# A two-layer decoder trunk on one core: layer 0's embedding gate as seven block products instead of eight

## The chip, the cores and the metric

The kernel runs on one core of one Trainium2 chip, in one launch. The metric is the time of a run on the device in microseconds (us); a kernel's time is the median of its runs.

## The reference, cut to what matters

512 tokens of width 1024 pass two layers. Each layer has a mixer (attention with a short convolution in layer 0, gated linear attention in layer 1), a gated MLP with a causal convolution, and a last stage that adds a gated projection of a per-layer input `p[i]` (512 x 256). All is float32.

```python
def _per_layer_embedding(x, p_i, norm, w_gate, w_proj):
    gate = jax.nn.sigmoid(_rms_norm(x, norm) @ w_gate)      # 512x1024 @ 1024x1024
    return gate * (p_i @ w_proj)                            # 512x256 @ 256x1024
...
    x = x + _conv_ffn(_rms_norm(x, ffn_norm[i]), ...)       # up 1024 -> 5632, down 2816 -> 1024
    x = x + _per_layer_embedding(x, p[i], ple_norm[i], ple_w_gate[i], ple_w_proj[i])
```

## The kernel before, in words

**Layout.** The residual `xT` is kept transposed: eight tiles `xT[0..7]` of 128 features by 512 tokens. A product of float32 numbers is made of three TensorE matmuls: every operand is split into a high part (a copy rounded to the matmul's type, on ScalarE) and a low part (the rest, a subtraction on VectorE), and high x high, high x low and low x high are summed in PSUM (`mm3`; `split` and `cut` make the parts). The factor 1/rms of a token is the same for all features, so it is applied after the product (`R`, 1/rms spread over 128 partitions). The sum of squares is gathered in `acc` (a square on ScalarE, an addition on VectorE, by feature tile), then `end_norm` turns it by four PE transposes, reduces it on VectorE and takes the root on GpSimd (`r`), and `spread` turns `r` back by four transposes into `R`.

**Seven products.** The MLPs already use Strassen's scheme in places: with weights cut in 2 x 2 blocks by even and odd feature tile and by column tile, and tokens cut in two halves of 256, the product of a pair of output tiles takes seven block products instead of eight. `seven(...)` is a generator with four steps: step 1 makes the product with `e1` (even features, left tokens) and copies it into both results X and Y; step 2 makes the ones with `s1`, `o1`, `s2`; step 3 the one with `s3`; step 4 those with `s4` and `o2`. Each of the seven is `product`: 4 j x 3 matmuls of 256 columns. `s1` to `s4` are sums of token halves, and on the weight side `seven_forms` makes the sums: it cuts the plain blocks (`plain`), subtracts in place, cuts the result (`t13`), subtracts, cuts a narrow one (`t2`, into two buffers of the tag `sq`, of which there are two), subtracts; step 3 cuts the last one (`last`, from `od`).

**The first MLP** (`ffn`, with its pool `fp`) ends with `down`, the down-projection, in units of two output tiles. On TensorE its order is written out (`manual_schedule`); the other engines' orders are chosen by a scheduler at compile time, which takes the ready instruction that comes first in the program. When the tiles of a unit are final, `finish(m)` is called for them. In layer 0 that was `advance`: split `gain * xT[m]` into `xg[m]`, and add its square to `acc`. In layer 1 it is `blocks`: it scales two tiles, forms `e1`, `o1`, `o2` and `s1` to `s4` of the pair, and splits them. Unit 3 is last; after the units 0 to 2 are final, 84 matmuls of 512 columns of it are left.

**The last stage of layer 0** (`ple0`) had a pool of its own. For each of four pairs of output tiles it cut a panel of `ple_w_gate` and one of `ple_w_proj`, made 2 x 8 x 3 matmuls of 512 columns for the gate and 2 x 2 x 3 for the projection, multiplied by `R`, took the sigmoid, multiplied, added to `xT` and called `advance` with the next layer's gain. Its TensorE order was left to the scheduler. The next mixer begins with products of `xg` with `gla_w_in` (`Values`), and these too are left to the scheduler.

Of the kernel before, what the change touches and what calls it, by code (L numbers as in the profile page):

```python
# [63 lines left out]
class Kernel:  # L64
# [228 lines left out]
    def blocks(self, m, gain, scratch, tags):  # L293


        nc = self.nc
        H = S // 2
        gx = scratch()
        nc.scalar.activation(gx, self.xT[m], AF.Copy, scale=gain[:, m : m + 1])

        def parts(x):
            w = x.shape[1]
            h, l = self.pair(self.fp, *tags)
            self.split((h[:, :w], l[:, :w]), x)
            return lambda b, c: (h[:, b * H + c * P : b * H + (c + 1) * P], l[:, b * H + c * P : b * H + (c + 1) * P])

        if m % 2 == 0:
            self.even = gx
            self.e1 = parts(gx[:, :H])
        else:  # L310
            e, o = self.even, gx
            op = parts(o)
            s12, s34 = scratch(), scratch()
            nc.vector.tensor_tensor(s12[:, :H], e[:, H:], o[:, H:], ALU.add)
            nc.vector.tensor_tensor(s12[:, H:], s12[:, :H], e[:, :H], ALU.subtract)
            s12p = parts(s12)
            nc.vector.tensor_tensor(s34[:, :H], e[:, :H], e[:, H:], ALU.subtract)
            nc.vector.tensor_tensor(s34[:, H:], o[:, :H], s12[:, H:], ALU.subtract)
            s34p = parts(s34)
            e1 = self.e1  # L320
            at = lambda f, b: lambda c: f(b, c)
            self.forms.append(
                dict(e1=at(e1, 0), o1=at(op, 0), o2=at(op, 1), s1=at(s12p, 0), s2=at(s12p, 1), s3=at(s34p, 0),
                     s4=at(s34p, 1))
            )
        self.squares(m)

# [459 lines left out]
    def operand(self, m, gain, tags):  # L787
# [19 lines left out]
            self.forms.append([(out[:, q, c], out[:, q + 1, c]) for q in (0, 2) for c in (slice(0, H), slice(H, S))])  # L807
        self.squares(m)

    def by_parity(self, raw):  # L810

        rv = raw.rearrange("p (j u) n -> p j u n", u=2)
        return rv[:, :, 0], rv[:, :, 1]
# [46 lines left out]
        nc.vector.tensor_tensor(b21, b21, b11, ALU.subtract)  # L860
        return t2

    def seven(self, od, ws, xg, forms, keep=True):

        nc = self.nc
        H = S // 2
        mm = nc.tensor.matmul
        W, V = self.pa(), self.pa()[:, :H]  # L870
        X, Y = self.ps(), self.ps()
        plain, t13, t2 = ws

        def product(out, w, c, x, first=False):
            kw = dict(skip_group_check=True)
            for j in range(ND // 2):
                (wh, wl), (xh, xl) = w(j, c), x(j)
                mm(out, wh, xh, start=first and j == 0, stop=False, **kw)  # L878
                mm(out, wh, xl, start=False, stop=False, **kw)  # L879
                mm(out, wl, xh, start=False, stop=j == ND // 2 - 1, **kw)  # L880

        def tokens(u, half):
            c = slice(half * H, (half + 1) * H)
            return lambda j: (xg[2 * j + u][0][:, c], xg[2 * j + u][1][:, c])

        s1, s2, s3, s4 = (lambda j, q=q: forms[j][q] for q in range(4))
        left, right = slice(0, H), slice(H, S)
# [4 lines left out]
        product(V, t13, 0, s1, True)  # L892
        more = V
        if keep:
            more = self.sp.tile([P, S], F32, tag="acc", name=self.nm("more"), bufs=1)[:, :H]
            nc.scalar.copy(more, V)
        product(X[:, left], plain, 1, tokens(1, 0))
        product(Y[:, left], t2, 0, s2)
        yield nc.scalar.copy(X[:, right], Y[:, left])
        last = self.cut_blocks(od)  # L900
        product(X[:, right], t13, 1, s3)
        yield nc.scalar.copy(Y[:, right], X[:, right])
        product(Y[:, left], last, 1, s4)
        product(X[:, right], last, 0, tokens(1, 1))
        yield X, Y, more

    def ffn(self, i, project, next_gain):
# [8 lines left out]
        with tc.tile_pool(name=f"ffn{i}", bufs=1) as fp:  # L916
# [47 lines left out]
            def prepare(d, behind=None):  # L964
# [11 lines left out]
                return self.seven(od, ws, xg, self.forms), w0, column(values[0], 0)  # L976

            def begin(d, steps, w):

# [64 lines left out]
            self.begin_norm(mine)  # L1044
            self.forms = []
            xg = self.xg
            ready = []

            def done(m, ps):
# [41 lines left out]

                close()
            self.begin_norm(mine)
            finish = lambda m: self.advance(m, next_gain)
            if i == 1:
                self.forms = []
                halves = []

                def half():
                    if not halves:  # L1100
                        x = both()
                        halves.extend([x[:, 0], x[:, 1]])
                    return halves.pop(0)

                self.half = half
                finish = lambda m: self.blocks(m, next_gain, half, mine if m < 4 else other)
            work = [lambda f=f: split_blocks(f) for f in (14, 16, 18, 20)]
            for f in (8, 10, 12):
                split_pair(f)
            self.down(i, acts, down_forms, both, work, finish, copied)  # L1110
            if i == 0:
                self.end_norm()
            else:
                self.ple1(fp)

    def down(self, i, acts, forms, both, work, finish, copied):
# [10 lines left out]
        if i == 0:  # L1127
            plan += [(2, "A", 0, 4, 3), (2, "A", 4, 6), (3, "B", 0, 4), (3, "B", 4, 8), (3, "A", 0, 3), (3, "A", 3, 6)]
            loads = ["B0", "A0", "A1", "B1", "C0", "B2", "C2", "A2", "B3", "A3"]
            inner = ["C1", "C3"]  # L1130
        else:
            plan += [(2, "A", 0, 3), (2, "A", 3, 6), (3, "B", 0, 4), (3, "B", 4, 8)]
            plan += [(3, "C", 0, 4), (3, "C", 4, 8), (3, "A", 0, 3), (3, "A", 3, 6)]
            loads = ["B0", "A0", "A1", "B1", "C0", "B2", "C2", "A2", "B3", "C3", "A3"]
            inner = ["C1"]
        blocked = 4 - i
        plan = [p if len(p) == 5 else p + (None,) for p in plan]
        got, cuts, gens, pending = {}, {}, {}, []
# [36 lines left out]
        def more_forms(u):  # L1175
# [1 line left out]
            t13 = self.cut_blocks(ev)  # L1177

            def rest():
                gens[u] = self.seven(od, (plain, t13, self.more_forms(ev, od)), acts[14:], forms, False)  # L1180

            pending.append(rest)

# [123 lines left out]
            out.append(hl)  # L1307
        return out

    def ple0(self, next_gain):  # L1310
        nc, a = self.nc, self.a
        with self.tc.tile_pool(name="ple0", bufs=1) as pool:
            xg, R, pT = self.xg, None, None
            wg = a["ple_w_gate"][0].rearrange("(k p) n -> p k n", p=P)
            wp = a["ple_w_proj"][0].rearrange("(k p) n -> p k n", p=P)
            self.begin_norm(("b0", "b1"))

            def finish(m2, w, gates):
                for c in range(2):
                    m, s = m2 + c, gates[c]  # L1320
                    pj = self.ps()
                    for k in range(2):
                        self.mm3(pj, w(k, c * P, (c + 1) * P), pT[k], start=k == 0, stop=k == 1)
                    nc.vector.tensor_tensor(s, s, pj, ALU.mult)
                    nc.vector.tensor_tensor(self.xT[m], self.xT[m], s, ALU.add)
                    self.advance(m, next_gain)

            late = None
            for m2 in range(0, ND, 2):
                g = self.weights(wg[:, :, m2 * P : (m2 + 2) * P], ND, 256)  # L1330
                w = self.weights(wp[:, :, m2 * P : (m2 + 2) * P], 2, 256)
                gates = []
                for c in range(2):
                    pg = self.ps()
                    for k in range(ND):
                        self.mm3(pg, g(k, c * P, (c + 1) * P), xg[k], start=k == 0, stop=k == ND - 1)
                    gates.append(pg)
                if R is None:
                    R = self.spread()
                    pT = self.load_p(0, pool)  # L1340
                for c in range(2):
                    s = pool.tile([P, S], F32, tag="pg", name=self.nm("pg"), bufs=4)
                    nc.vector.tensor_tensor(s, gates[c], R, ALU.mult)
                    nc.scalar.activation(s, s, AF.Sigmoid)
                    gates[c] = s
                if late:
                    finish(*late)
                late = (m2, w, gates)
            finish(*late)
            self.end_norm()  # L1350

    def ple1(self, fp):

# [35 lines left out]
        def add(banks, form, ws, first=False, order=None):  # L1389
# [2 lines left out]
            kw = dict(skip_group_check=True)  # L1392
            both = (0, H)
            for j, i, (c0, c1), o in order or [(j, i, both, banks[i]) for j in range(J) for i in range(2)]:
                lh, ll = forms[j][form](i)
# [607 lines left out]
```

## Time and profile before

| | us |
|---|---|
| runs (3) | 1200.00, 1200.26, 1201.72 |
| median | 1200.26 |
| profiled execution, first to last instruction | 1199.4 |
| of it, down-projection's end, units 0 to 2 final to the last matmul | about 501 to 520.5 |
| layer 0's last stage on TensorE | 520.5 to 576.7 |

The page gives the profiled execution by its span; 0.9 us lie between this span and the median of the runs. Times "at" a number below are us from the span's start. PE is the TensorE's matmuls, PEld its weight loads, DVE VectorE, ACT ScalarE, POOL GpSimd, SP the engine that issues most DMAs. A matmul's own time in the trace overlaps the next one's, so PE's pace is read from the distance of starts.

### The profile page before, as it was taken

What the parts mean: (1) busy time and instruction counts of PE and PEld (TensorE: products, weight loads), DVE (VectorE), ACT (ScalarE), POOL (GpSimd) and SP (SyncE); (2) the same over time, 40 slices, a digit from 0 to 9 for tenths busy, and PEclk for the clock granted to TensorE, in tenths of its full rate; (3) what the DMA queues carried; (4) which work ended last, traced back from release to release, by engine and by line L of the source; (5) the groups of instructions that cost most, each with busy time, mean ns of one, the idle gap of its engine ahead of it and who ended that gap; (6) DMA issues with size and microseconds to landing.
All of it is one profiled execution on the core that took longest, in us unless ns stands there. A gap on an engine that the chain in (4) does not pass through costs nothing.

```text
span 1199.4 us, 19840 instructions
## 1 busy us (share of the span) xinstructions
PE 1192.4 (99%) x8074; PEld 1076.9 (90%) x8074; DVE 966.4 (81%) x1543; ACT 671.1 (56%) x1093; POOL 44.8 (4%) x64
## 2 busy tenths in 40 slices
PE   9999999999999999999999999999999999999998
PEld 8877789999999989888988988899999999888887
DVE  6786687898999986746679876687989999988595
ACT  7466565655565753534563655555555656655374
POOL 2610000000000000000100000000000000000000
PEclk9999999999999999999999999999999999999999
DMA  7232222333332342232322222223233333322601
GB/s 223 72 97 80 74 88 71 106 106 106 106 107 89 113 138 84 87 106 86 107 93 70 75 68 70 88 72 115 97 112 100 106 106 114 124 89 98 210 1 71
DMA packets 113216, 117.74 MB, mean 98 GB/s; under 512 B 2873, under 2 KB 108403, under 8 KB 113125
## 3 DMA queue, kind: packets, MB, share of 16 engines
q1 hardware_dynamic: 111760, 115.35, 29.5%
q8 instruction: 63, 1.03, 0.4%
q0 software_dynamic: 560, 0.42, 0.3%
q10 hardware_dynamic: 804, 0.70, 0.2%
q14 instruction: 29, 0.23, 0.1%
HBM read 114.37 MB, written 2.10 MB: 97 GB/s over the span
## 4 chain that ended last, share of the span: by engine, by line
PE 92%; DVE 5%; ACT 1%; DMA 1%; issue 0%; ACTq 0%; DVEq 0%
PE ps L169 14%; PE ps L170 14%; PE ps L171 14%; PE pa L170 7%; PE pa L171 7%; PE pa L169 7%; PE ps L878 5%; PE ps L880 5%; PE ps L879 5%; PE pa L878 2%; PE pa L880 2%; PE pa L879 2%; PE ps L1400 1%; PE ps L1398 1%; PE ps L1399 1%; DVE wl L150 1%
## 5 line engine op out<-in xcount | busy, mean ns | idle before, releaser
L149 ACT ACTIVATE wh<-raw 128x1024 fp32r<-128x1024 f32 (+4 forms) x154 | 152.5, 992 | 128.9 <-PE ps L170 92.8
L150 DVE TENSOR_TENSOR wl<-raw,wh 128x1024 fp32r<-128x1024 f32 (+4 forms) x154 | 175.3, 1140 | 57.9 <-ACT wh L149 57.0
L825 ACT ACTIVATE wh<-raw 128x1024 fp32r<-128x1024 f32 x78 | 83.0, 1064 | 115.8 <-DVE raw L850 75.9
L937 DVE SCALAR_TENSOR_TENSOR zt<-z,vfa,zt 128x510 f32<-128x510 f32 (+1 forms) x176 | 131.0, 745 | 0.3
L826 DVE TENSOR_TENSOR wl<-raw,wh 128x1024 fp32r<-128x1024 f32 x78 | 95.4, 1222 | 12.8 <-ACT wh L825 12.8
L171 PE MATMUL pa<-b,wl 128*128 128x256 f32 x352 | 97.3, 276 | 0.1
L171 PE MATMUL pa<-a,wl 128*128 128x256 f32 x352 | 97.2, 276 | 0.0
L169 PE MATMUL pa<-b,wh 128*128 128x256 f32 x352 | 97.2, 276 | 0.0
L169 PE MATMUL pa<-a,wh 128*128 128x256 f32 x352 | 97.2, 276 | 0.0
L170 PE MATMUL pa<-b,wh 128*128 128x256 f32 x352 | 97.2, 276 | 0.0
L170 PE MATMUL pa<-a,wh 128*128 128x256 f32 x352 | 97.2, 276 | 0.0
L935 ACT ACTIVATE zt<-z,vfb 128x512 f32<-128x512 f32 x88 | 71.5, 813 | 19.6 <-DVE z L927 9.5
L169 PE MATMUL ps<-b,wh 128*128 128x512 f32 x192 | 76.6, 399 | 0.0
L170 PE MATMUL ps<-b,wh 128*128 128x512 f32 x192 | 75.1, 391 | 0.0
L171 PE MATMUL ps<-b,wl 128*128 128x512 f32 x192 | 75.0, 391 | 0.0
L171 PEld LDWEIGHTS pa<-b,wl 128*128 128x128 f32 x352 | 66.1, 188 | 0.3 <-DVE wl L150 0.3
L169 PEld LDWEIGHTS pa<-b,wh 128*128 128x128 f32 x352 | 66.1, 188 | 0.0
L170 PEld LDWEIGHTS pa<-a,wh 128*128 128x128 f32 x352 | 66.1, 188 | 0.0
L169 PEld LDWEIGHTS pa<-a,wh 128*128 128x128 f32 x352 | 66.1, 188 | 0.0
L170 PEld LDWEIGHTS pa<-b,wh 128*128 128x128 f32 x352 | 66.1, 188 | 0.0
L171 PEld LDWEIGHTS pa<-a,wl 128*128 128x128 f32 x352 | 66.1, 188 | 0.0
L878 PE MATMUL ps<-four,wh 128*128 128x256 f32 x232 | 64.7, 279 | 0.0
(472 smaller groups left out, 3667.7 us busy)
## 6 DMA issues: line engine op xcount, KB each, us to landing
raw<-in_ffn_w_up_dram SPq DMA_DIRECT2D x42, 1024.0 KB, 5.1
raw<-in_ffn_w_down_dram SPq DMA_DIRECT2D x13, 1024.0 KB, 4.8
raw<-in_hy_w_in_dram SPq DMA_DIRECT2D x8, 1024.0 KB, 5.0
raw<-in_gla_w_in_dram SPq DMA_DIRECT2D x8, 1024.0 KB, 5.1
raw<-in_ffn_w_down_dram SPq DMA_DIRECT2D x8, 768.0 KB, 4.1
raw<-in_ple_w_gate_dram SPq DMA_DIRECT2D x6, 1024.0 KB, 4.6
raw<-in_hy_w_out_dram SPq DMA_DIRECT2D x16, 256.0 KB, 3.9
raw<-in_gla_w_out_dram SPq DMA_DIRECT2D x4, 1024.0 KB, 4.7
```

Source lines behind the costliest of these rows:

```text
L149: nc.scalar.activation(hv, v, AF.Copy)
L150: self.rest_cut = nc.vector.tensor_tensor(lv, v, hv.bitcast(F32), ALU.subtract)
L169: mm(out, lh, rh, start=start, stop=False, **kw)
L170: mm(out, lh, rl, start=False, stop=False, **kw)
L171: mm(out, ll, rh, start=False, stop=stop, **kw)
L825: nc.scalar.activation(h, src, AF.Copy)
L826: nc.vector.tensor_tensor(l, src, h.bitcast(F32), ALU.subtract)
L878: mm(out, wh, xh, start=first and j == 0, stop=False, **kw)
L879: mm(out, wh, xl, start=False, stop=False, **kw)
L880: mm(out, wl, xh, start=False, stop=j == ND // 2 - 1, **kw)
L935: nc.scalar.activation(y, z, AF.Identity, scale=w2[:, f : f + 1], bias=bb[:, f : f + 1])
L937: nc.vector.scalar_tensor_tensor(out=y[:, tap:], in0=z[:, : S - tap], scalar=w[:, f : f + 1], in1=y[:, tap:], op0=ALU.mult, op1=ALU.add,)
```

## The change: what it does

Layer 0's gate is now computed by `seven`, four groups of two output tiles. `finish` is `blocks` in both layers, so the sums of x are made at the end of the down-projection; `ple0` is called inside `ffn`, uses the pool `fp`, and has its TensorE order written out. `proj` and the turning of `p` (`load_p`) come first, then the groups; `p` is loaded through SP in two halves before the stage (it was one load through ScalarE's queue). All of `ple_w_proj` is loaded and split once. The split of the new `xT` for the next mixer (`enter`) moves from each group to the last one, because its buffers (`b0`, `b1`) hold sums of x until then. `end_norm` stands in group 0 after step 2, `spread` after step 3. `seven` takes its operands by name and a function for the buffer that keeps V; for the MLPs this is only another way of writing.

```diff
@@ blocks @@
-            return lambda b, c: (h[:, b * H + c * P : ...], l[:, b * H + c * P : ...])
+            return [(h[:, c], l[:, c]) for c in HALVES]
...
+                dict(e1=self.e1[0], o1=op[0], o2=op[1], s1=s12p[0], s2=s12p[1], s3=s34p[0], s4=s34p[1])
@@ seven @@
-        product(W[:, left], plain, 0, tokens(0, 0), True)
+        product(W[:, left], plain, 0, x["e1"], True)
...
-        if keep:
-            more = self.sp.tile([P, S], F32, tag="acc", ...)[:, :H]
+        if keep is not None:
+            more = keep()
@@ ffn, behind the up-projection @@
-            finish = lambda m: self.advance(m, next_gain)
-            if i == 1:
-                ...
+            finish = lambda m: self.blocks(m, next_gain, half, mine if m < 4 else other)
...
             if i == 0:
-                self.end_norm()
+                self.ple0(fp, both, self.g_mix[1])
@@ ple0 @@
+        pin = self.p_halves(0)
+        steps = prepare(load(0))          # panel by SP; plain, t13, t2; seven(...)
+        wj_raw = self.raw(2, D)
+        nc.sync.dma_start(wj_raw, a["ple_w_proj"][0].rearrange("(k p) n -> p k n", p=P))
+        wj = [... two tiles of the tag "four" ...]
+        for c in (slice(0, D // 2), slice(D // 2, D)):
+            self.split([w[:, :, c] for w in wj], wj_raw[:, :, c])
...
+        def enter(*ms):
+            for m in ms:
+                hl = self.pair(self.fp, "b0", "b1")
+                self.split(hl, self.xT[m], next_gain[:, m : m + 1])
+                self.xg.append(hl)
+
+        with tc.manual_schedule(engines={ET.PE}):
+            pT = self.load_p(0, fp, pin)
+            pjs = [proj(0), proj(1)]
+            for g in range(groups):
+                ends = g + 1 == groups
+                if not ends:
+                    raw = load(g + 1)
+                next(steps)
+                if ends:
+                    enter(0, 1)
+                next(steps)
+                if ends:
+                    enter(2, 3)
+                if g == 0:
+                    self.end_norm()
+                    self.begin_norm(None)
+                else:
+                    pjs = [proj(2 * g)]
+                next(steps)
+                if g == 0:
+                    R = self.spread()
+                else:
+                    pjs.append(proj(2 * g + 1))
+                last = steps
+                if not ends:
+                    steps = prepare(raw)
+                X, Y, more = next(last)
+                if ends:
+                    enter(4, 5)
+                gates = both()
+                h2 = lambda x: x.rearrange("p (u t) -> p u t", u=2)
+                nc.vector.tensor_tensor(gates[:, 0], X, R, ALU.mult)
+                s = gates[:, 1]
+                nc.vector.tensor_tensor(h2(s), h2(Y), more.unsqueeze(1).to_broadcast([P, 2, H]), ALU.add)
+                nc.vector.tensor_tensor(s, s, R, ALU.mult)
+                for c in range(2):
+                    m, s = 2 * g + c, gates[:, c]
+                    nc.scalar.activation(s, s, AF.Sigmoid)
+                    nc.vector.tensor_tensor(s, s, pjs[c], ALU.mult)
+                    nc.vector.tensor_tensor(self.xT[m], self.xT[m], s, ALU.add)
+                    self.squares(m)
+            enter(6, 7)
+        self.end_norm()
@@ run @@
-        self.ple0(self.g_mix[1])
```

More of the change, by code (lines that the diff above doesn't have):

```diff
@@ L808, in operand, with aside @@
         self.squares(m)
+    def aside(self):
+        return self.sp.tile([P, S], F32, tag="acc", name=self.nm("more"), bufs=1)[:, : S // 2]
     def by_parity(self, raw):
@@ L861, in more_forms, with tokens_and_forms, seven @@
         return t2
-    def seven(self, od, ws, xg, forms, keep=True):
+    def tokens_and_forms(self, xg, forms, first=0):
+        part = lambda u, c: lambda j: tuple(x[:, c] for x in xg[first + 2 * j + u])
+        s1, s2, s3, s4 = (lambda j, q=q: forms[j][q] for q in range(4))
+        left, right = HALVES
+        return dict(e1=part(0, left), o1=part(1, left), o2=part(1, right), s1=s1, s2=s2, s3=s3, s4=s4)
+    def seven(self, od, ws, x, keep=None):
         nc = self.nc
@@ L880, in product @@
                 mm(out, wl, xh, start=False, stop=j == ND // 2 - 1, **kw)
[L882 to L887, printed above, removed]
-        product(W[:, left], plain, 0, tokens(0, 0), True)
+        left, right = HALVES
+        product(W[:, left], plain, 0, x["e1"], True)
         nc.scalar.copy(X[:, left], W[:, left])
@@ L975, in prepare @@
                 values.append(load_values(d))
-                return self.seven(od, ws, xg, self.forms), w0, column(values[0], 0)
+                return self.seven(od, ws, operands, self.aside), w0, column(values[0], 0)
             def begin(d, steps, w):
@@ L1046, in ffn @@
             xg = self.xg
+            operands = self.tokens_and_forms(xg, self.forms)
             ready = []
@@ L1093, in ffn, with half @@
             self.begin_norm(mine)
-            finish = lambda m: self.advance(m, next_gain)
-            if i == 1:
[L1096 to L1106, printed above, removed]
+            self.forms = []
+            halves = []
+            def half():
+                if not halves:
+                    x = both()
+                    halves.extend([x[:, 0], x[:, 1]])
+                return halves.pop(0)
+            self.half = half
+            finish = lambda m: self.blocks(m, next_gain, half, mine if m < 4 else other)
             work = [lambda f=f: split_blocks(f) for f in (14, 16, 18, 20)]
@@ L1308, in load_p @@
         return out
[L1310 to L1318, printed above, removed]
-                for c in range(2):
[L1320 to L1350, printed above, removed]
```

46 lines of the change are left out of this document (32 added, 14 removed).

## The prediction

> **What bounds the kernel now.** I read the page first: the span, each engine's busy share and the chain that ended last.
>
> ```profile
> span 1199.4 us, 19840 instructions
> ...
> PE 1192.4 (99%) x8074; PEld 1076.9 (90%) x8074; DVE 966.4 (81%) x1543; ACT 671.1 (56%) x1093; POOL 44.8 (4%) x64
> ...
> PE 92%; DVE 5%; ACT 1%; DMA 1%; issue 0%; ACTq 0%; DVEq 0%
> ```
>
> The chain is PE's for 92% of the span. So matmul time removed is worth its full price, but only if PE does not wait in exchange. The busy time of stretches shows how things stand around the change: the end of the down-projection, and the old last stage.
>
> ```profile
> 490.00:520.50 30.50, 30.50 (x163) 26.22 (x162) 17.50 (x22) 14.60 (x22) 0.00 (x0) 1.00 0.23 73
> 520.50:576.70 56.20, 56.20 (x257) 46.61 (x256) 34.19 (x50) 26.26 (x38) 1.01 (x1) 1.00 0.32 105
> ```
>
> The columns are the stretch, its length, and busy time of PE, PEld, DVE, ACT and POOL, then the granted clock, which is full. PE is busy throughout both: the old stage has no wait to win back, and every wait of the new one is a loss. DVE has 13 us free in the first stretch and 22 us in the second.
>
> **The change part by part.** First, what PE no longer does. The groups by line, in the window of the old stage, count the gate's matmuls (the same x64 on lines 170 and 171), and the order of time gives the paces.
>
> ```profile
> L169 PE MATMUL ps<-a,wh 128*128 128x512 f32 x64 | 25.1, 392 | 0.0
> ...
> L111 ACT ACTIVATE a<-xT,vec 128x512 fp32r<-128x512 f32 x2 | 1.4, 711 | 0.0
> ```
>
> ```profile
> 520.49 0.39 PE L169 MATMUL ps<-a,wh 128*128 128x512 f32 x1
> ...
> 524.57 0.33 PE L333 MATMUL pa<-cf,acc 128*128 128x128 f32 x1
> ```
>
> ```profile
> 489.09 0.28 PE L878 MATMUL ps<-four,wh 128*128 128x256 f32 x1
> ...
> 490.45 0.28 PE L878 MATMUL ps<-a,t 128*128 128x256 f32 x1
> ```
>
> 18 matmuls of 512 columns lie between the first two starts: 4.08/18 = 0.2267 us each. 12 of 256 columns (one block product of the down-projection) lie between the others: 1.36/12 = 0.1133, half of it. The old gate was 192 x 0.2267 = 43.5 us. The new one is 4 groups x 7 products x 12 x 0.1133 = 38.1. **Saved on PE: 5.4 us.** The projection (48 matmuls) and the sixteen transposes (p, the sums, R) stay.
>
> This half price is the premise. The Trainium skill ("TensorE: Matmul & The Clock Gate", section "Back-to-back issue gap") says otherwise: a stream of load-and-multiply pairs runs at about 131 ns per matmul at 512 columns and 81 at 128, so halving the columns would save far less than half. By its ratio (an estimate: 98 at 256 columns, by interpolation on that page) the new gate would cost 57 us and the change would lose 13. The measured pace contradicts it here, and the sum goes by the pace.
>
> Second, the waits. The new stage's PE order is fixed, so whatever its next instruction waits for holds up all that is queued behind it.
>
> *The head.* The first PE work is now the turning of p, then the projection of tiles 0 and 1, which need p split. The old stage did this in its middle, behind other matmuls. Rows in order of time, of that place and of the down-projection's end:
>
> ```profile
> 520.01 1.37 DVE L1209 TENSOR_TENSOR xT<-xT,ps 128x512 f32<-128x512 f32 x2 [1.31 <-PE ps L171]
> ...
> 520.46 0.63 ACT L149 ACTIVATE wh<-raw 128x512 fp32r<-128x512 f32 x1 [3.02 <-PE ps L170]
> ...
> 532.30 1.04 PE L1304 MATMUL pa<-cf,pin 128*128 128x128 f32 x8
> ...
> 533.33 1.09 ACT L108 ACTIVATE ph<-pa 128x512 fp32r<-128x512 f32 x2
> ...
> 534.13 1.28 DVE L109 TENSOR_TENSOR pl<-pa,ph 128x512 fp32r<-128x512 f32 x2
> ```
>
> With ACT and DVE nearly free, the first low part was done 534.13 + 0.69 - 532.30 = 2.5 us after the transposes began. PE has about 0.8 us of transposes and one matmul on the high part (0.23) in that time, so it waits at least 1.5 us. At the other end, work that comes earlier in the program goes first. Tiles 6 and 7 are final at 521.4 (first row). Their two scaled copies (0.71 each, the L111 row), the splits of `e1` and `o1` (half and full width, about 0.4 and 0.6), and the cut of `last` (about 1.06), whose buffer comes free when the 0.63 us cut of the second row could start, put about 3 us on ACT ahead of p, and `s12`, `s34` and their low parts stand ahead on DVE. Then the low part of p is ready at about 526.4 instead of 523, and PE waits 5.0 us. I take 3.3, the middle: DVE will run late here (below), which delays tiles 6 and 7 themselves and lets p's high parts slip in front. What these waits cover in return is the pair's own sums: they would otherwise hold up the products with `e1` and `s1`. That is free only because of this wait.
>
> *The sums of squares.* `t2` takes both `sq` buffers, and the squares of tiles 6 and 7 come after it, so they wait for step 2's last product. The MLP's start has the same pattern:
>
> ```profile
> 189.81 1.16 ACT L290 ACTIVATE sq<-xT 128x512 f32<-128x512 f32 x2 [0.35 <-PE ps L879]
> ...
> 190.63 1.48 DVE L291 TENSOR_TENSOR acc<-acc,sq 128x512 f32<-128x512 f32 x2
> ...
> 192.39 0.60 PE L333 MATMUL pa<-cf,acc 128*128 128x128 f32 x4
> ...
> 194.01 1.04 POOL L179 TENSOR_TENSOR rtok<-rs,mhalf 128x4 f32<-128x4 f32 x1 [58.48 <-DVE rs L178]
> ```
>
> The squares start when the PE releases them, and `acc` is done at 192.11, 2.3 us later. There 24 matmuls of the value columns filled the time. In the new group 0 the transposes of `acc` follow step 2 directly: PE waits 2.4 us, or nothing if the squares get the buffers before `t2`. I take 2.4, since `t2` can be made before tiles 6 and 7 are final.
>
> *The root.* From the transposes' start to `r` it took 195.05 - 192.39 = 2.7 us. The new order has the transposes (0.36) and step 3 (1.36) in between: PE waits 1.0 us before `spread`.
>
> *DVE.* Rows of one piece each, from the up-projection (groups by line) and a queued pair (order of time):
>
> ```profile
> L826 DVE TENSOR_TENSOR wl<-raw,wh 128x1024 fp32r<-128x1024 f32 x36 | 44.0, 1222 | 4.2 <-ACT wh L825 4.2
> ...
> L800 DVE TENSOR_TENSOR four<-four 128x256 f32<-128x256 f32 x4 | 1.7, 418 | 0.0
> ```
>
> ```profile
> 547.61 1.29 DVE L1325 TENSOR_TENSOR xT<-xT,pg 128x512 f32<-128x512 f32 x2
> ```
>
> Two queued pieces of 512 take 1.29, so one occupies 0.60 in a queue and 0.69 alone; 1024 take 1.13 and 1.22. A group has three wide cuts, and fourteen pieces of 512: four weight differences, one narrow cut, seven in the tail (X and Y to `xT`), two squares. Queued that is 3 x 1.13 + 14 x 0.60 = 11.8 us, beside 84 x 0.1133 + 12 x 0.2267 = 12.2 us on PE. So DVE just fits, with PE waits here and there: 0.2 for groups 1 to 3. The old `advance` is out of groups 0 to 2, and `enter` (8 pieces) falls into the last group and behind it, where `Values` products with tiles 0 to 5 cover it, and the two free banks of X and Y of group 2 let them start: 0.2. Before the stage, sums for tiles 0 to 5 add 3 x (5 x 0.42 + 3 x 0.69 - 2 x 0.69) = 8.3 us (the last two are the old low parts), the first panel 4 x 0.69 more than the old cuts, and the projection's weights 2 x 1.22: 17.5 + 13.5 = 31.0 us in 30.5. No PE work of the down-projection waits for it (its cuts come first in the program), but the head meets a late DVE.
>
> *DMA.* SP issues the two halves of p first; the second waits for the buffer in which activation 7's low part lies. Queued behind it are the first panel and the projection's weights.
>
> ```profile
> raw<-in_ple_w_gate_dram SPq DMA_DIRECT2D x6, 1024.0 KB, 4.6
> ```
>
> After that part is read, 36 matmuls x 0.2267 = 8.2 us remain. If the panel really queues behind, two loads of 4.6 and a cut of 2.3 end 3 us late, inside the long head; if it is asked for when its buffer comes free, they cost nothing. I take nothing.
>
> The sum: -5.4 + 3.3 + 2.4 + 1.0 + 0.4 = **+1.7 us** on the 1199.4 us span, so 1201.1; the median of the runs lies 0.9 above the span: **1202.0**.
>
> **The rivals.**
>
> 1. *Covered.* The squares get `sq` first and the head is at its short end: -5.4 + 1.5 + 1.0 + 0.2 = -2.7, so 1197.6 (1194.9 if PE's work alone counted). For it speaks that DVE is late, which can push `t2` behind the squares; against it the MLP's start, where `t2` was first. Chance 0.22.
> 2. *Long head.* The pair's chain and the cut of `last` go before p: 5.0 instead of 3.3, +3.4, so 1203.7. It is measurably slower than before from a head of 4.0 us on. For it speaks the program order; against it that ACT idled 3.02 us before 520.46. Chance 0.20.
> 3. *DVE becomes the bound.* If pieces come singly, waiting for PE or ACT, a group costs 3 x 1.22 + 14 x 0.69 = 13.3 us, 1.1 over PE's 12.2, in three groups: +3.2 more, 1205.2. Against it: in the old stage's tail the pieces did queue (the pair of 1.29). Chance 0.09.
> 4. *The clock.* At the start of the kernel PE was slow after idling:
>
> ```profile
> 1.31 3.36 PE L204 MATMUL pa<-ones_r 128*128 128x512 f32 x7 [1.31 <-DVE mhalf L193]
> 4.47 1.05 PE L470 MATMUL ps<-cf,xin 128*128 128x128 f32 x4
> ```
>
> Seven matmuls took 3.16, 0.45 each, twice the pace: 1.6 us lost. If the long head sets PE back in this way, 1205.3. The Trainium skill ("TensorE: Matmul & The Clock Gate", Part 1) has a rule for it: an idle window of about 3.4 us halves the clock until PE has been busy as long. No row here shows it in mid-kernel. Chance 0.05.
>
> 5. *Half-width matmuls at the pace of their weight loads.* A load takes 188 ns, 336 of them 63.2 us, 20 more than the old gate: about 1220. The 0.1133 pace speaks against it, and the skill's issue-gap rule above is its only support. Chance 0.02.
>
> **How the numbers follow.** The forecast, 1202.0, has 0.42. For this kernel about 0.2% (2.4 us) is what a measurement tells from no change, so "same" is 1197.9 to 1202.7. Faster: most of rival 1, 0.20. Same: the rest of it, most of the forecast, a little of rival 2: 0.40. Slower: the forecast's upper part and rivals 2 to 5, 0.40. The forecast's own range is 1200.0 to 1203.5. The range to hold 8 in 10 takes in rival 1 nearly to PE's work alone and rivals 2 to 4: 1196.5 to 1206.0.
>
> **What would show it.** Right: gate matmuls 336 at 0.1133; PE idle 2 to 5 us before the first projection matmul, released by the low part of p; 2 to 3 us before the transposes of `acc`, released by DVE; about 1 us before those of `r`, released by POOL; next to nothing in groups 1 to 3. Wrong: squares of tiles 6 and 7 that run before step 2 ends (then 2.4 us less); transposes of p found among the down-projection's matmuls (then the head costs nothing); waits for `wl`, `t` or `raw` in groups 1 to 3 (DVE); `Values` starting late behind the stage.

## The result and the profile after

The changed kernel takes 1211.32 us (median of 4 runs, 1211.22 to 1212.7) against 1200.96 (4 runs, 1200.0 to 1201.72) for the kernel before beside it: ratio 1.0087, 95% interval 1.0073 to 1.0101. The forecast was 1202.0, and the time lies above the top of its range. The profiled execution grew from 1199.4 to 1209.5. Its page, the lines that answer to those shown of before, and the granted clock by slices:

```profile
span 1209.5 us, 20223 instructions
...
PE 1192.0 (99%) x8218; PEld 1081.0 (89%) x8218; DVE 993.3 (82%) x1593; ACT 691.6 (57%) x1135; POOL 45.3 (4%) x64
...
PEclk9999999999999999989999999999999999999999
...
PE 60%; issue 29%; DVE 7%; ACT 2%; DMA 1%; POOL 0%; ACTq 0%; POOLq 0%; DVEq 0%
```

PE's busy time hardly fell, although 5.4 us of gate work are gone: one slice has a lower clock, in which the same matmuls count longer. It is the slice of the changed stage. By stretches (the end of the down-projection, the head of the stage, the rest of it):

```profile
490.00:520.50 30.50, 30.50 (x163) 26.15 (x162) 26.39 (x44) 21.65 (x34) 0.00 (x0) 1.00 0.33 104
...
520.20:534.10 13.90, 6.73 (x22) 4.88 (x21) 10.71 (x19) 6.67 (x12) 0.00 (x0) 0.66 0.36 117
534.10:586.80 52.70, 49.53 (x383) 46.69 (x382) 42.05 (x60) 31.25 (x54) 1.43 (x1) 0.99 0.19 60
```

The down-projection is as long as before, its PE full, though DVE does 26.4 us there in place of 17.5. The stage runs from 520.2 to 586.8: 66.6 us, where the old one took 56.2. These 10.4 us are the whole difference, and most of them are in the first 13.9 us, for which the profile lists only 22 matmuls and transposes.

**The head**, PE in order of time. What is in brackets is idle time and who ended it:

```profile
520.23 1.03 PE L1305 MATMUL pa<-cf,pin 128*128 128x128 f32 x8
525.21 0.79 PE L169 MATMUL pa<-four,four 128*128 128x512 f32 x1 [3.95 <-ACT four L108]
529.23 0.79 PE L170 MATMUL pa<-four,four 128*128 128x512 f32 x1 [3.23 <-DVE four L109]
529.82 0.63 PE L171 MATMUL pa<-four,four 128*128 128x512 f32 x1
...
533.66 0.63 PE L171 MATMUL pa<-four,four 128*128 128x512 f32 x1
534.09 0.41 PE L884 MATMUL pa<-a,wh 128*128 128x256 f32 x1
```

The head's work is 0.8 for the transposes of `p` and 12 x 0.2267 = 2.7 for the projection, 3.5 us. It takes 534.09 - 520.23 = 13.9, so **10.4 us are lost**. By starts, less the work in between: 4.2 before the first projection matmul (for p's high part), 3.8 before the second (for its low part), and the other 2.4 because the matmuls after that follow at (533.66 - 529.82)/9 = 0.427 us, half pace. Who held up `p` stands in VectorE's and ScalarE's rows:

```profile
520.18 1.28 DVE L1210 TENSOR_TENSOR xT<-xT,ps 128x512 f32<-128x512 f32 x2
...
524.61 0.69 DVE L826 TENSOR_TENSOR t<-raw,t 128x512 fp32r<-128x512 f32 x1
525.22 1.29 DVE L109 TENSOR_TENSOR b<-zt,b 128x512 fp32r<-128x512 f32 x2
...
526.75 1.22 DVE L109 TENSOR_TENSOR four<-raw,four 128x1024 fp32r<-128x1024 f32 x1
...
528.49 1.29 DVE L109 TENSOR_TENSOR four<-pa,four 128x512 fp32r<-128x512 f32 x2
```

```profile
521.58 0.61 ACT L290 ACTIVATE sq<-xT 128x512 f32<-128x512 f32 x1
...
523.54 0.62 ACT L825 ACTIVATE t<-raw 128x512 fp32r<-128x512 f32 x1
...
524.58 0.58 ACT L108 ACTIVATE four<-pa 128x512 fp32r<-128x512 f32 x1
```

Behind the last additions to `xT`, VectorE worked without a gap for 8.3 us, and p's two low parts (`four<-pa`) were the last two of 15 pieces: behind the last pair's sums, the sums of squares, `t2` (`t<-raw`), the low parts of the pair's forms (`b<-zt`), and half of the cut of W_p, the projection's weights (`four<-raw`). p's first high part (`four<-pa` on ScalarE) was done at 525.16, so its low part stood 3.3 us in VectorE's queue. TensorE meanwhile stood at the second matmul of its written order. The clock by stretches (it is the third number from the end):

```profile
524.50:524.80 0.30, 0.00 (x0) 0.00 (x0) 0.30 (x2) 0.30 (x2) 0.00 (x0) 0.55 0.00 0
...
525.20:529.20 4.00, 0.79 (x1) 0.29 (x1) 4.00 (x8) 2.43 (x4) 0.00 (x0) 0.50 0.01 2
...
534.70:535.00 0.30, 0.30 (x5) 0.30 (x3) 0.00 (x0) 0.00 (x0) 0.00 (x0) 0.88 1.09 389
```

It falls to half at 524.53 and is full again at 534.77 (the shares 0.55 and 0.88 of their 0.3 us give these points).

**The root**, on PE, VectorE and GpSimd:

```profile
540.87 0.28 PE L886 MATMUL ps<-a,wl 128*128 128x256 f32 x1
...
541.89 0.28 PE L886 MATMUL ps<-b,wl 128*128 128x256 f32 x1
543.81 0.65 PE L348 MATMUL pa<-cf,rtok 128*128 128x128 f32 x4 [1.64 <-POOL rtok L179]
```

```profile
540.88 0.68 DVE L339 TENSOR_REDUCE ss<-pa 128x4 f32<-128x512 f32 x1
541.48 0.68 DVE L849 TENSOR_TENSOR raw<-raw 128x512 f32<-128x512 f32 x1
542.08 0.17 DVE L178 TENSOR_SCALAR rs<-ss 128x4 f32<-128x4 f32 x1
```

```profile
542.32 1.43 POOL L179 TENSOR_TENSOR rtok<-rs,mhalf 128x4 f32<-128x4 f32 x1 [347.63 <-DVE rs L178]
```

1.8 us lost. A weight difference (L849, 0.60 in the queue) slipped between the sum and the small step to `rs`.

**The borders of the groups.** Between groups 0 and 1, on PE and on ScalarE:

```profile
549.66 0.28 PE L886 MATMUL pa<-b,wl 128*128 128x256 f32 x1
550.81 0.39 PE L884 MATMUL ps<-a,wh 128*128 128x256 f32 x1 [0.87 <-ACT ps L890]
```

```profile
547.87 1.28 ACT L1391 ACT_TABLE_LOAD   x1
549.17 1.32 ACT L1391 ACTIVATE zt<-zt 128x512 f32<-128x512 f32 x2
550.39 0.36 ACT L890 COPY ps<-pa 128x256 f32<-128x256 f32 x1
```

The copy of W that the next product adds to stands behind group 0's sigmoids, and these behind the load of their table: 1.0 us. Three other starts of a product behind such copies lose 0.25 to 0.7 us each (1.2 in sum); the largest, before 581.17, waits for a copy (L900) that stands behind two squares.

### The profile page after: what moved, and what is told of

It reads as the page before. It is cut to its first block, busy times and chain, and to the rows that moved or that the text cites. A ratio compares the mean times of both kernels' runs of the same rounds, so it can differ in the third digit from the quotient of the medians.

```text
span 1209.5 us, 20223 instructions
## 1 busy us (share of the span) xinstructions
PE 1192.0 (99%) x8218; PEld 1081.0 (89%) x8218; DVE 993.3 (82%) x1593; ACT 691.6 (57%) x1135; POOL 45.3 (4%) x64
## 3 DMA queue, kind: packets, MB, share of 16 engines
q8 instruction: 64, 1.05, 0.4%
## 4 chain that ended last, share of the span: by engine, by line
PE 60%; issue 29%; DVE 7%; ACT 2%; DMA 1%; POOL 0%; ACTq 0%; POOLq 0%; DVEq 0%
PE ps L169 10%; PE ps L171 10%; PE ps L170 10%; PE pa L170 4%; PE pa L171 4%; PE pa L169 4%; PE ps L884 3%; PE ps L886 3%; PE ps L885 3%; DVE wl L150 1%; PE ps L1446 1%; PE ps L1445 1%; PE ps L1444 1%; PE pa L886 1%; DVE wl L826 1%
## 5 line engine op out<-in xcount | busy, mean ns | idle before, releaser
L150 DVE TENSOR_TENSOR wl<-raw,wh 128x1024 fp32r<-128x1024 f32 (+4 forms) x142 | 163.0, 1149 | 41.6 <-ACT wh L149 41.1
L149 ACT ACTIVATE wh<-raw 128x1024 fp32r<-128x1024 f32 (+4 forms) x142 | 141.4, 998 | 87.1 <-PE ps L170 55.5
L825 ACT ACTIVATE wh<-raw 128x1024 fp32r<-128x1024 f32 x90 | 95.8, 1065 | 125.1 <-DVE raw L850 76.1
L826 DVE TENSOR_TENSOR wl<-raw,wh 128x1024 fp32r<-128x1024 f32 x90 | 110.2, 1224 | 28.9 <-ACT wh L825 28.8
```

The costliest lines, as they stand in the source:

```text
L149: nc.scalar.activation(hv, v, AF.Copy)
L150: self.rest_cut = nc.vector.tensor_tensor(lv, v, hv.bitcast(F32), ALU.subtract)
L825: nc.scalar.activation(h, src, AF.Copy)
L826: nc.vector.tensor_tensor(l, src, h.bitcast(F32), ALU.subtract)
```

## The experiments

**Theory A**: nearly all of it is the order of the queues at the head: TensorE's fixed order stands at the projection, whose operand is last in a long VectorE queue, and idling then halves the clock. **Theory B**: seven products need more from VectorE and ScalarE than they can give at this place, so the loss comes back wherever it is taken away. The ratios below are to the kernel before, run beside each, with 95% intervals.

**e1_free.** TensorE's order in the stage is left to the scheduler.

```diff
-        with tc.manual_schedule(engines={ET.PE}):
+        with nullcontext():
```

> The changed kernel, with the last stage's TensorE order left to the scheduler instead of written out. Theory A (the head: PE's fixed order waits 8 us for p's low part, which stands behind the last pair's sums and the projection's weights on DVE, and then runs 11 matmuls at half pace; 10.3 us lost of 15): other gate products that are ready go first, the wait shrinks to about 3 us and the time to 1202 to 1205 us. Theory B (ACT and DVE can't feed seven products, wherever the wait stands): the wait only moves, 1208 or more.

Measured: 1211.24 us, 1.0088 (1.0073 to 1.0103). A miss for A as it was put. The scheduler chose almost the same order (two matmuls on p's high parts go ahead of the first one on a low part, in place of one), and the two waits of the head are there as before, now 5.01 and 2.80:

```profile
527.10 1.22 PE L169 MATMUL pa<-four,four 128*128 128x512 f32 x2 [5.01 <-ACT four L108]
531.11 0.79 PE L170 MATMUL pa<-four,four 128*128 128x512 f32 x1 [2.80 <-DVE four L109]
```

So writing the order out is not the cause: left to itself, the scheduler too put the projection first. The first wait is longer for another reason: the load of W_p took 6.4 us in this execution (5.4 in the changed kernel's), and ScalarE waited 1.23 for it before it cut W_p.

**e2_late.** `p` is turned after step 1 of group 0, tile 0 is projected after step 2 (behind the sums of squares), tile 1 after step 3, and the root is spread after that.

```diff
-            pT = self.load_p(0, fp, pin)
-            pjs = [proj(0), proj(1)]
...
+                if g == 0:
+                    pT = self.load_p(0, fp, pin)
...
+                pjs = [proj(2 * g)]
                 next(steps)
+                pjs.append(proj(2 * g + 1))
```

> The changed kernel, with p turned after step 1 of group 0 and the projection of tiles 0 and 1 after steps 2 and 3, as in the later groups; spread after it. Theory A: PE now waits for the last pair's own sums, about 2 us in step 1 and 1 to 2 in step 2, at full pace, and the projection covers most of the 1.8 us before R is spread: 1201 to 1203.5 us. Theory B: the same DVE queue is met by other products, 1208 or more.

Measured: 1201.97 us, 1.0011 (1.0002 to 1.002), as A expected. 9.4 of the 10.4 us are gone. What is left on PE at the head (in sum 2.7 by starts) and between groups 0 and 1:

```profile
522.58 0.38 PE L884 MATMUL pa<-b,wh 128*128 128x256 f32 x1 [1.04 <-ACT b L108]
523.41 0.39 PE L885 MATMUL pa<-b,wh 128*128 128x256 f32 x1 [0.45 <-DVE b L109]
...
526.58 0.39 PE L885 MATMUL pa<-b,wh 128*128 128x256 f32 x1 [0.61 <-DVE b L109]
...
541.64 0.38 PE L884 MATMUL ps<-a,wh 128*128 128x256 f32 x1 [0.69 <-ACT ps L890]
```

Now the last pair's own parts (`b`) are waited for, as the prediction said of a head without that cover, and the root is covered by the projection.

**e3_early.** The order stays as changed, but `p` and W_p are loaded after step 10 and turned and split after step 12 of the down-projection (into free buffers of the tags `z` and `four`).

```diff
+                hooks = {10: p_load, 12: p_split}
+            self.down(i, acts, down_forms, both, work, finish, copied, hooks)
...
-            pT = self.load_p(0, fp, pin)
             pjs = [proj(0), proj(1)]
```

> The changed kernel, with p and the projection's weights loaded, turned and split during unit 3 of the down-projection (p in two z buffers, the weights in one four), the projection of tiles 0 and 1 still first. Theory A: the projection runs at once at 0.2267 us a matmul, about 1.5 us of wait for the last pair's sums follow, the 1.8 us before R is spread stay: about 1202.5 us. Theory B: 1208 or more. It also shows whether the down-projection bears the extra DVE work (no wait of PE there) or not.

Measured: 1202.67 us, 1.0018 (1.0009 to 1.0028). The projection ran at once, as A expected. The down-projection bore the extra VectorE work with no wait on PE, which speaks against B. What stays at the head are waits of 0.8 and 1.7 for the last pair's parts.

**e4_fill.** 70 matmuls of 256 columns, without use, between p's turning and the projection.

```diff
...
+            for _ in range(70):
+                nc.tensor.matmul(fill[:, :H], forms[0]["e1"][0][:, :P], forms[0]["e1"][0], start=True, stop=True, ...)
             pjs = [proj(0), proj(1)]
```

> The changed kernel, with 70 matmuls of 256 columns added between the turning of p and the projection, into a bank that nobody reads (7.9 us of PE work in the 8 us of waits). If the half pace of the first projection matmuls comes from PE's idling, they run at 0.2267 us again and the time falls by about 2.3 us to 1209, though PE does more. If it has another cause, 1211.3 or more.

Measured: 1208.08 us, 1.0062 (1.0045 to 1.0079): 3.2 us faster than the changed kernel, though PE does 70 x 0.1133 = 7.9 us more. The projection on PE:

```profile
528.78 0.40 PE L169 MATMUL pa<-four,four 128*128 128x512 f32 x1
...
531.52 0.28 PE L884 MATMUL pa<-a,wh 128*128 128x256 f32 x1
```

12 matmuls in 2.74: full pace, although the projection started only after 528, as before. The half pace came from PE's idling.

**e7_first.** One line: p's high parts (on ScalarE) and low parts (on VectorE) get priority. TensorE's order is instruction for instruction the changed kernel's, and all the work is there.

```diff
-            self.split(hl, ps)
+            with self.tc.high_priority(offset=300) if given else nullcontext(): self.split(hl, ps)
```

> The changed kernel with one edit: p's high and low parts go ahead of the last pair's sums in the scheduler's order (a priority), so that the two low parts stand directly behind the first sum on VectorE instead of at the end of some 8 us of queue. TensorE's order is the same instruction for instruction, and VectorE has the same work. Theory A: the projection starts at about 523.5 in place of 525.2 and goes on at once, at full pace (no second wait, so no idle TensorE and no half pace); the last pair's forms come later by 1.3 us. The head falls from 10.3 us lost to 5 to 7: 1206.5 to 1208.5. Theory B: the order in the queue does not matter, the sum of the work does; 1210.5 to 1212.

Measured: 1202.96 us, 1.0018 (1.0009 to 1.0027). **8.4 of the 10.4 us hang on p's place in these two queues.** PE, then VectorE:

```profile
522.25 0.50 PE L169 MATMUL pa<-four,four 128*128 128x512 f32 x1 [0.86 <-ACT four L108]
523.09 0.50 PE L170 MATMUL pa<-four,four 128*128 128x512 f32 x1 [0.34 <-DVE four L109]
...
525.73 0.28 PE L884 MATMUL pa<-a,wh 128*128 128x256 f32 x1
```

```profile
522.36 1.28 DVE L109 TENSOR_TENSOR four<-pa,four 128x512 fp32r<-128x512 f32 x2
```

The low parts are made at 522.36 in place of 528.49, PE waits 1.1 and 0.6 by starts, the clock stays full, and the head ends at 525.73 in place of 534.09. It was better than expected: the last pair's parts, put back by 1.3 us, lay behind the projection's 2.7 and cost PE only 0.8.

**e5_table** (e2_late with a four-element Sigmoid on `r` behind the first `end_norm`, so that the table is loaded early) and **e6_both** (e5_table with `p` and W_p brought in as in e3_early):

```diff
                     self.end_norm()
+                    nc.scalar.activation(self.few(NT, "rs", 4), self.r, AF.Sigmoid)
```

> The late order (e2_late) with one more line: a four-element Sigmoid on r right after the first end_norm, so that ScalarE loads the sigmoid's table while it idles and not between group 0 and group 1. Theory A: the 1.3 us that TensorE waits at that border in e2_late (0.44 + 0.86) come from the table load (1.28 us) ahead of the copies W -> X, Y; so they go, 1201.97 - 1.0 to 1.3 = 1200.7 to 1201.0. Theory B (ScalarE and VectorE have too much work at each border): the wait stays at about 1 us, 1201.6 to 1202.2.

> The late order, the early table load, and p and W_p brought in after t=10 and turned and split after t=12 of the down-projection. Nothing is then queued on VectorE at the head but the last pair's parts and sums and the panel's forms. Theory A: the head's 1.2 + 0.72 + 0.8 us of e2_late fall to 0.5 to 1.5, the root's wait is covered by the projection; 1198.5 to 1200.0, below the kernel before (the seven products' saving of 5.4 less some 4 us of waits). Theory B: the work on VectorE is the same in sum, only earlier, and the down-projection or the borders of the groups pay for it; 1201.5 to 1203.

Measured: e5_table 1202.51 us, 1.0016 (1.0007 to 1.0025); e6_both 1202.61 us, 1.0018 (1.0009 to 1.0027). Both missed A's gain; e6_both lies where B expected it, e5_table above both. The wait for the copies at the border of groups 0 and 1 (0.86 by starts in e2_late) is gone in both, which fits what was said of the table load; but in e5_table a wait for a low part of W in the product before it is 1.05, where e2_late has 0.44. And in both profiled executions the clock fell at the head. The granted clock of e5_table, then of e6_both:

```profile
524.30:524.60 0.30, 0.01 (x1) 0.00 (x0) 0.30 (x2) 0.30 (x2) 0.00 (x0) 0.56 0.00 0
...
527.70:528.00 0.30, 0.30 (x4) 0.30 (x4) 0.30 (x2) 0.30 (x1) 0.00 (x0) 0.92 0.00 0
```

```profile
521.90:524.40 2.50, 1.00 (x6) 0.61 (x6) 2.50 (x6) 2.50 (x6) 0.00 (x0) 1.00 0.00 0
524.40:524.70 0.30, 0.30 (x5) 0.30 (x5) 0.30 (x1) 0.30 (x1) 0.00 (x0) 1.00 0.00 0
524.70:525.00 0.30, 0.30 (x4) 0.30 (x3) 0.30 (x1) 0.30 (x2) 0.00 (x0) 0.50 0.00 0
...
531.30:531.60 0.30, 0.30 (x3) 0.30 (x3) 0.04 (x1) 0.23 (x1) 0.00 (x0) 0.62 1.02 358
```

Half clock from 524.34 to 527.75 and from 524.70 to 531.53. This is not the whole reason, though: not every execution has it. Of e6_both's eleven, five have a mean granted clock of 1.0 and take 1201.66 to 1202.61 us, five have 0.997 and take 1203.34 to 1204.47 (one has 0.998: 1202.42). So the fall costs some 2 us where it comes, but e6_both misses A's 1198.5 to 1200.0 without it too. The waits for the last pair's parts stayed: 1.22 and 0.72, then 0.9 at half clock, where e2_late has 1.20, 0.72 and 0.80; so they did not come from p and W_p.

In e5_table the queues at the head stand in e2_late's order. What was late is the load of W_p: 6.8 us against 5.0, and ScalarE waited for it before it could cut W_p:

```profile
518.72 2.01 ACT L108 ACTIVATE four<-raw 128x1024 fp32r<-128x1024 f32 x2 [1.63 <-DMA raw<-in_ple_w_proj_dram]
```

In e2_late this cut begins at 517.20. All that is queued behind it, the last additions to `xT` too, came some 1.3 us later, and PE's first wait at the head was 2.8 instead of 1.2. This profiled execution is the longest of e5_table's eleven (1204.54). Eight of the others have a mean clock of 0.999 or 1.0, and their median is 1202.8: they missed the gain as well, and for them no trace shows why.

**e8_best** (`p` early, tile 0 projected at the head, tile 1 behind the sums of squares, the Sigmoid fed from the last pair's `s4`) and **e9_first** (e7_first with the last two of these edits):

```diff
+                    nc.scalar.activation(self.few(NT, "rs", 4), forms[3]["s4"][0][:, :NT].bitcast(F32), AF.Sigmoid)
                     self.end_norm()
                     self.begin_norm(None)
+                    pjs.append(proj(1))
```

> p and W_p brought in early as in e6_both; projection of tile 0 at the head, where TensorE waits for the last pair, projection of tile 1 directly behind the sums of squares, where it waits for the root; the four-element Sigmoid reads the last pair's s4, so that the table load comes behind the last pair's parts and not beside the root. Theory A: e2_late's 2.7 us at the head fall to 1 or less (1.36 us of projection lie there now), the root to 0 to 0.5, the border of groups 0 and 1 to 0 to 0.3 as in e6_both, and TensorE waits nowhere long enough for the clock to fall: 1197.5 to 1199.5, faster than the kernel before. Theory B (the work comes back as a wait somewhere): 1201 to 1203.

> e7_first (p's parts ahead in the queues) with two more edits: the projection of tile 1 directly behind the sums of squares, and the four-element Sigmoid that reads the last pair's s4. Theory A: of e7_first's 1202.96 the border of groups 0 and 1 gives back 1.4 to 1.7 us (table load 1.28 ahead of the copies), the root 0.55, and the head costs up to 1 more since only one projection covers the last pair: 1200.7 to 1202.0. Theory B: no gain, 1202.5 to 1203.5.

Measured: e8_best 1205.8 us, 1.004 (1.0028 to 1.0053), a miss for both theories; e9_first 1201.73 us, 1.0007 (0.9998 to 1.0016), as A expected. In e8_best PE waited 2.0 for a high part of the last pair's `s1` (ScalarE) and 1.2 for its low part, since the squares, `t2` and a wide cut were put ahead of them on both engines, and the clock was halved again.

**e10_parts** (e8_best with the squares of tiles 6 and 7, `t2` and the last cut tied behind the last pair's parts), **e11_gate** (and each group's sigmoids behind the next group's copies of W) and **e12_spread** (e10_parts with the root spread behind group 0's last products, and the sigmoids of group 2 alone moved as in e11_gate):

```diff
+    def behind(self, instructions):      # this block's instructions queue behind these, engine by engine
...
+        with self.behind(behind):        # more_forms: the last pair's s1, s2; the last cut: s3, s4
             with self.tc.high_priority(offset=40):
                 t2 = self.cut_blocks(b11, False)
...
-                if g == 0:
-                    R = self.spread()
...
                 X, Y, more = next(last)
+                if g == 0:
+                    R = self.spread()
```

> e8_best with the order of VectorE's and ScalarE's queues at the head tied down: the squares of tiles 6 and 7 and the first panel's t2 come behind the high and low parts of the last pair's s1 and s2, the panel's last cut behind those of s3 and s4. Theory A: e8_best's waits at the head (0.52, 2.04, 1.23 and 1.5 of half pace after them) came from t2 (0.69), a cut (1.23) and the sums of squares (0.68 each) that stood ahead of the last pair's low parts on VectorE; they fall to under 1 in sum, and the clock does not fall: 1205.8 - 4 to 5 = 1200.5 to 1202. Theory B: the same work only waits elsewhere, 1204 to 1206.

> e10_parts, and each group's two sigmoids behind the next group's copies of W (ScalarE), so that those copies never stand behind a sigmoid (0.62) or a table load. Theory A: the waits at the borders of the groups in e8_best (0.49, 0.22, 1.13, 0.23) go but for 0.1 to 0.2 each: 1.5 less than e10_parts, 1199.0 to 1200.5, below the kernel before. Theory B: the same as e10_parts within 0.3, since the gates then come later and the next group or the stage behind it waits for them.

> e10_parts with two edits: the root is spread behind the last two products of group 0 (2.7 us of TensorE work) instead of ahead of them, and the sigmoids of group 2 and the last stage's first two parts come behind group 3's copies of W. Theory A: e10_parts waits 1.65 for the root and 1.11 at the border of groups 2 and 3; the first goes whole, the second to 0.3: 1201.7 - 2.0 to 2.5 = 1199.2 to 1199.7, below the kernel before by 0.1%. Theory B: each wait taken away comes back at the next border (the gates of group 0 come later), 1201.0 to 1202.0.

Measured: e10_parts 1201.7 us, 1.0007 (0.9998 to 1.0016); e11_gate 1202.35, 1.0013 (1.0004 to 1.0022); e12_spread 1200.92 against 1201.18, 0.9997 (0.9988 to 1.0006). e10_parts did what A said of it: 4.1 us less than e8_best, by order alone. e11_gate gave nothing (0.65 us more than e10_parts): the wait between groups 2 and 3 fell from 1.1 to 0.3, but waits of 0.5, 0.3 and 0.3 stand elsewhere, where e10_parts has 0.35 and 0.24, as B has it. e12_spread came out between the two expectations. PE's largest waits in e10_parts, then those in e12_spread:

```profile
534.91 0.65 PE L356 MATMUL pa<-cf,rtok 128*128 128x128 f32 x4 [1.48 <-POOL rtok L184]
...
567.10 0.38 PE L893 MATMUL ps<-a,wh 128*128 128x256 f32 x1 [0.94 <-ACT ps L899]
```

```profile
533.20 0.39 PE L893 MATMUL ps<-a,wh 128*128 128x256 f32 x1 [0.50 <-ACT ps L912]
...
552.47 0.39 PE L893 MATMUL ps<-a,wh 128*128 128x256 f32 x1 [0.71 <-ACT ps L899]
```

Both named waits went. Two new ones came, for copies on ScalarE: by starts 0.7, where the root's wait had stood before, and 0.9 between groups 1 and 2. e12_spread's profiled execution is 1197.8, 1.6 under the kernel before, but the medians differ by 0.3, and the interval holds 1. No version was measurably faster than the kernel before.

What the runs settle: A, for 8.4 (e7_first) to 9.4 (e2_late) of the 10.4 us. The rest is open in part. With the head in order some 3.5 (e12_spread) to 5 us (e10_parts) of waits by starts stay, spread over ScalarE's copies, the last pair's parts and the root, and they use up most of the 5.4 us that the seven products save. That a wait taken away comes back at another place, as B says, was seen in e11_gate and, for 1.6 of the 2.8 us taken away, in e12_spread. That VectorE and ScalarE have too much work for the seven products was not shown: in the 52.7 us behind the changed kernel's head they were busy 42.05 and 31.25 us. Whether an order exists that hides all these waits was not found out.

## Why the prediction was wrong, point by point

- **The gate, -5.4.** Right: 9 matmuls of 256 columns from 540.87 to 541.89 are 0.1133 each. The issue-gap rule of the Trainium skill ("TensorE: Matmul & The Clock Gate", section "Back-to-back issue gap"), by which, as the prediction estimated, the change would have lost 13 us, is not borne out.
- **The head, +3.3 with a bound of 5.0. This is the step that failed**: 10.4, and some 0.3 more in the gate's first matmuls, until the clock came back. The mechanism was right (PE waits for p's low part, behind the last pair), its size was not. The prediction summed ScalarE's queue ahead of `p`, about 3 us, and only named the pieces on VectorE (`s12`, `s34` and their low parts) without adding them up. They, `t2`, half of W_p's cut, a weight difference and the sums of squares were 7.0 us without a gap ahead of p's low parts. ScalarE's sum was near (3.6 us from its first scaled copy to p's first high part); VectorE's queue made the low part wait 3.3 us more. The "middle" between 1.5 and 5.0 had no row behind it, and the reason given for it, that a late VectorE lets p's high parts slip in front, looked at the wrong half: the high part alone lets one matmul run.
- **Rivals 2 and 4** were set up as alternatives and came together: the long head (8.0 of waits) and, because of it, the clock (2.4, and the 0.3). The prediction had seen half pace in a row of the kernel's start, priced it at 1.6 us and gave it 0.05, because no row showed it in mid-kernel. All four runs of the changed kernel have a mean granted clock of 0.995 or 0.996, against 0.999 in the profile before: behind waits of 4.2 and 3.8 it was no separate chance.
- **The squares, +2.4.** Wrong, 0: they ran at 521.58 and before `t` at 523.54, which the prediction had named as the sign.
- **The root, +1.0.** 1.8: 0.6 for the weight difference in VectorE's queue, and 1.43 on GpSimd where the row used had 1.04.
- **VectorE and the end, +0.4.** The down-projection bore its share (26.4 us busy, where 31.0 were forecast: the rest came at the head), and no group waited long for VectorE. But the borders cost 2.2 (1.0 and 1.2), from ScalarE: its copies of W stand behind sigmoids, a table load and squares. The prediction priced VectorE's pieces by group and never ScalarE's order there.
- **DMA, 0.** Right for the changed kernel: none of PE's waits in the stage is for a load, and ScalarE waited 0.16 for W_p. But the load of W_p was only just in time: in e5_table, where it took 6.8 us in place of 5.4, the head came later by it.

The sum as measured: -5.4 + 10.4 + 0.3 + 1.8 + 2.2, and 0.3 for two of the next stage's matmuls that now lie inside: 9.6 of the stage's 10.4. The rest is PE's slower first matmuls behind each wait, about 0.1 each.

## What to carry to other kernels

When an engine with a fixed order gets a new first operand, add up all that is queued ahead of that operand on *every* engine it passes, not on the nearest one; a queue of small pieces was most of the loss here, and one priority took back four fifths of it. Long waits of TensorE can cost twice, as waits and as half pace behind them: waits of 4.2 and 3.8 us did so in all four runs, behind waits of 1.2 and 0.7 us the clock fell in e6_both's profile and stayed full in e2_late's. A saving of 5 us by shorter matmuls came to nothing because the new hand-overs between the products were not all covered: those that were not cost 0.2 to 1.1 us each.

## What the runs showed of the hardware

In the profiled executions half clock came in multiples of one length: 10.24 us in the changed kernel (524.53 to 534.77), 6.83 in e6_both, 3.41 in e5_table: three, two and one times 3.41. In the changed kernel a single matmul of 0.23 us between two waits (at 525.21) did not bring the full clock back, and after the idling PE worked at half clock for 5.5 more us (529.23 to 534.77).

Full idleness is not needed: in the 3.41 us ahead of e6_both's fall at 524.70, PE was busy for 1.91 us. Nor is the busy time alone what decides: e2_late has the same two waits (1.20 and 0.72, 1.92 us busy in the 3.41 us from 521.00), and its clock stayed full; e3_early was busy for only 1.35 us of the 3.41 from 525.20, and its clock stayed full as well; and e6_both's own executions differ, as told above. A window of fixed length whose start does not depend on the kernel would explain all of this, but no run here shows where its borders lie. The Trainium skill ("TensorE: Matmul & The Clock Gate", Part 1) speaks of such a free-running window of about 3.4 us that decides; the lengths agree with it, while its "idle window" is too strict for e6_both.
